# Retention scores in three float32r passes instead of one plain float32 product

## The chip, the cores and the metric

The kernel runs on one core of a Trainium2 chip. The metric is the device time of one execution in microseconds (us), from the core's first instruction to its last with what lies around them. Three executions give a median; one more was recorded by the hardware profiler.

## The reference

A decoder trunk of two layers over 512 tokens with 1024 channels. Each layer has a token mixer with three branches (retention, a gated recurrence called HGRN2, a Conformer convolution) and a feed-forward part with a convolution. The change is in the retention branch: 4 heads of 128 channels; queries and keys are rotated by position, and a token's output is the sum over earlier tokens of score x decay x value.

```python
def _rope(t, positions):
    ...
    return jnp.concatenate([t1 * cos - t2 * sin, t1 * sin + t2 * cos], axis=-1)

def _retention(q, k, v):
    """o_t = sum_{s<=t} gamma_h^(t-s) (q_t.k_s) v_s."""
    ...
        scores = jnp.einsum('bhtd,bhsd->bhts', qc, kc) * decay_mask
        out = jnp.einsum('bhts,bhsv->bhtv', scores, vc)
```

All inputs and outputs are float32. The kernel computes the scores over all earlier tokens at once instead of chunk by chunk.

## The kernel before, in words

Everything is held transposed: 128 channels on the partitions, 512 tokens along the free axis. A projection (`proj`) multiplies eight 128x128 weight tiles with eight 128x512 tiles of the input. Weights and inputs are split into two float32r parts: a high part rounded by ScalarE (`AF.Copy` into a float32r tile) and a low part, the difference, computed by VectorE. `mm3` (lines 248 to 251) then makes one product of three passes, high x high, high x low and low x high, which accumulate in PSUM. `split` (lines 226 to 232) does this for an intermediate result; `prefetch` (lines 215 to 217) does it for each 512 KB chunk of weights, with four buffers for the high and four for the low parts.

The order of the work is written by hand. The main loop runs projections. Heads are generators in a list `heads`, other work in a list `fill`. After every fourth weight tile `proj` calls `tick`, which takes one step of each of up to three heads and then steps of `fill` as a credit of microseconds allows. A head's TensorE instructions are put behind the last projection matmul by `issue_after(last[0].ins)`, where `last[0]` is set by `mm3`. Within these limits a planner in the compiler orders each engine's instructions by planned times; on the chip each engine takes them in that order.

In each layer, after the convolution inputs, the list `MIX` sets the order: values for HGRN2, two HGRN heads, values for retention, and then HGRN and retention heads mixed, with retention heads 2 and 3 last. For a retention head the main loop projects and rotates q, then projects and rotates k (`rope`, lines 536 to 543: two ScalarE copies that swap the halves, three VectorE operations), projects the gate, and appends `ret_head` (lines 545 to 562). That loads the decay mask (line 547); four steps follow, for key blocks j = 0 to 3, each with a score product of 128 keys with the w = 512, 384, 256 or 128 tokens from the block on (line 553) and a VectorE multiplication by the mask (line 555). Then four products with the values (line 561) and `head_out` give the branch's output.

The matmuls of the score products have plain float32 operands; in the profile each such product has two matmul records and two weight loads. The 47 buffers named `b` (tag "B") are shared by all such intermediate tiles, and the score products use one of two PSUM buffers `ps`.

Of the kernel before, what the change touches and what calls it, by code (L numbers as in the profile page):

```python
# [2 lines left out]

# [1 line left out]

# [14 lines left out]
S = 512  # L20
# [69 lines left out]
def trunk(ctx, tc, xT, cT, pos, ada, bada, wts, cols, lbl, rope_c, decay, hmask, outT):  # L90
    nc = tc.nc
    mm = nc.tensor.matmul
# [18 lines left out]
    def big(dt=F32, w=S):  # L111
        return bp.tile([P, w], dt, tag="B", name=nm("b"), bufs=NB)
# [7 lines left out]
    def pm():  # L120
        return pp.tile([P, S], F32, tag="pm", name=nm("pm"), bufs=4)

    def ps():
        return pp.tile([P, S], F32, tag="ps", name=nm("ps"), bufs=2)

    def po():
        return pp.tile([P, S], F32, tag="po", name=nm("po"), bufs=2)
# [36 lines left out]
    last = [None]  # L164
# [55 lines left out]
    def chunk(kind, ahead=LA):  # L220
        prefetch(ahead + 1 - len(ready))
        k, w = ready.pop(0)
        assert k == kind, (k, kind)
        return w

    def split(src, hi=None):
        if hi is None:
            hi = big(F32R)
            act(hi, src, AF.Copy)  # L229
        lo = big(F32R)  # L230
        tt(lo, src, hi.bitcast(F32), ALU.subtract)  # L231
        return hi, lo
# [15 lines left out]
    def mm3(dst, a, b, first, end):  # L248
        mm(dst, a[0], b[0], start=first, stop=False)  # L249
        mm(dst, a[0], b[1], start=False, stop=False)  # L250
        last[0] = mm(dst, a[1], b[0], start=False, stop=end)  # L251

    def sl2(w, o, n=128):
        return [t[:, o:o + n] for t in w]

    def proj(w, xs, us=TK):
        q = pm()
        n = len(xs)
        for k in range(n):
            mm3(q, sl2(w, 128 * k), xs[k], k == 0, k == n - 1)  # L260
            if k % 4 == 3:
                tick(us)
        return q

    def proj_octo(hs):
        qs = [pm(), pm(), pm(), pm(), ps(), ps(), po(), po()]
        for kt in range(KT):
            w = chunk("octo", 0)
            for n in range(8):
                mm3(qs[n], sl2(w, 128 * n), hs[kt], kt == 0, kt == KT - 1)  # L270
        return qs

    def proj_quad(kind, hs, between):

        qs = [ps(), pm(), ps(), pm()]
        ws = []
        for hf, (a, b) in enumerate(HALVES):
            for c in range(4):
                if hf == 0:
                    ws.append(chunk(kind, 0))  # L280
                for k in range(2):
                    kt = 2 * c + k
                    for n in range(4):
                        mm3(qs[n][:, a:b], sl2(ws[c], 512 * k + 128 * n), sl2(hs[kt], a, b - a),
                            hf == 0 and kt == 0, hf == 1 and kt == KT - 1)
                if hf == 0 and c == 0:
                    between()
        return qs
# [137 lines left out]
    def head_out(l, o, gname, h, sg, out):  # L426
        sq = big()
        act(sq, o, AF.Square)
        u = big()
        stt(u, o, col(l, gname, h), sg, ALU.mult, ALU.mult)  # L430
        sq = exact2(sq)
        yield 0.6
        for v in colsum(*sq):
            yield 0.0
        r = rstd(v, 8.0)
        tt(u, u, r, ALU.mult)
        out[h] = split(u)
        yield 3.0
# [97 lines left out]
    def rope(q, CC, SS):  # L536
        sw, o = big(), big()
        act(sw[0:64, :], q[64:128, :], AF.Copy)
        act(sw[64:128, :], q[0:64, :], AF.Copy)
        tt(o, q, CC, ALU.mult)  # L540
        tt(sw, sw, SS, ALU.mult)
        tt(o, o, sw, ALU.add)
        return o

    def ret_head(l, h, q, k, sg, v, out):
        dm = big()
        nc.sync.dma_start(dm, decay[h])
        yield 0.0
        pt = []
        for j in range(4):  # L550
            w = S - 128 * j
            z = ps()
            mm(z[:, 0:w], k[:, 128 * j:128 * (j + 1)], q[:, 128 * j:S], start=True, stop=True)  # L553
            a = big(w=w)
            tt(a, z[:, 0:w], dm[:, 0:w], ALU.mult)
            pt.append(a)
            yield 0.1 + w / 960
        o = po()
        hs = slice(128 * h, 128 * (h + 1))
        for j in range(4):  # L560
            mm(o[:, 128 * j:S], v[j][:, hs], pt[j], start=j == 0, stop=j == 3)  # L561
        yield from head_out(l, o, "retg", h, sg, out)
# [174 lines left out]
    for l in range(L):  # L737
# [20 lines left out]
        for what, h in MIX:  # L758
            if what == "g" and h < 0:
                for g, tp, q in proj_tok(hs):  # L760
                    for t2 in range(2):
                        act(vg[2 * tp + t2][:, 256 * g:256 * (g + 1)], q[:, 256 * t2:256 * (t2 + 1)], AF.Copy)
            elif h < 0:
                for g, tp, q in proj_tok(hs):
                    qv = q.rearrange("p (t h d) -> p t h d", h=2, d=128)
                    sm = bp.tile([P, 4], F32, tag="sm", name=nm("sm"), bufs=2)
                    nc.vector.tensor_reduce(sm, q.rearrange("p (a d) -> p a d", d=128),
                                            mybir.AxisListType.X, ALU.add)
                    for t2 in range(2):
                        stt(vr[2 * tp + t2][:, 256 * g:256 * (g + 1)].rearrange("p (h d) -> p h d", d=128),  # L770
                            sm[:, 2 * t2:2 * t2 + 2].unsqueeze(2).broadcast_to([P, 2, 128]), -1.0 / 128,
                            qv[:, t2], ALU.mult, ALU.add)
            elif what == "g":
                qf = proj(chunk("in"), hs)
                qq = proj(chunk("in"), hs)
                qg = proj(chunk("in"), hs)
                drain(heads, 2)
                heads.append(hgrn_head(l, h, *hgrn_gates(l, h, qq, qf, qg), vg, u_b))
            else:
                q = rope(proj(chunk("in"), hs), *CS)  # L780
                k = rope(proj(chunk("in"), hs), *CS)
                qg = proj(chunk("in"), hs)
                sg = big()
                act(sg, qg, AF.Silu)
                drain(heads, 2)
                heads.append(ret_head(l, h, q, k, sg, vr, u_a))

        ys = [None] * 8
        for bi, b in enumerate(ORDER):
            us = (u_a, u_b, u_c)[b]  # L790
            for jp in range(4):
                sg = []
                for t in range(2):
                    q = proj(chunk("in"), hs, TG if bi == 2 else TK)
# [9 lines left out]
                w = chunk("br")  # L804
                for t in range(2):
                    j = 2 * jp + t
                    q = pm()
# [16 lines left out]
        w = [chunk("out", 2), chunk("out", 1), chunk("out", 0)]  # L824
# [50 lines left out]
        for j in range(8):  # L875
# [4 lines left out]
            for a, b in parts:  # L880
                q = pm()[:, a:b]
                for k in range(FT):
# [3 lines left out]
                    w = [h[1] for h in held if h[0] == ci][0]  # L886
# [127 lines left out]
```

## Time and profile before

| What | Value |
| --- | --- |
| Median of 3 runs | 1808.3 us (1806.86 to 1808.81) |
| Profiled execution | 1809.82 us, of which the span in the trace is 1808.0 us |
| Granted TensorE clock, mean over the span | 0.998 |
| TensorE matmul, busy | 1781.2 us (99%) |
| VectorE, busy | 1297.0 us (72%) |
| ScalarE, busy | 761.9 us (42%) |
| GpSimd, busy | 35.3 us (2%) |

PE is TensorE's matmuls, PEld its weight loads, DVE VectorE, ACT ScalarE, POOL GpSimd. A matmul's duration in the trace includes the time in which the next one has already started, so the spacing of starts, and not the duration, is what a matmul costs. The chain of work that ended last is followed back from the last instruction; each of its pieces has the time by which it moved the end. The retention heads run from about 180 to 310 us in layer 0 and from about 1070 to 1210 us in layer 1.

### The profile page before, as it was taken

To read this page: it belongs to the slowest core of one execution; us is meant where nothing else is said; L and a number is where in the kernel's file an instruction comes from. 1 tells how busy PE (TensorE), PEld (TensorE's weight loads), DVE (VectorE), ACT (ScalarE), POOL (GpSimd) and SP (SyncE) were. 2 spreads that over 40 slices of the span, in tenths; PEclk is the share of its full clock that TensorE was granted. 3 is DMA by queue.
4 is the path that set the end of the run, shared out by engine and by line. 5 is a ranking of instruction groups with operands and counts; after the bars stand their busy time and mean duration, and the time that the engine had idled before them with its cause. 6 is when DMAs were issued, how large, how long until landed. Compare 5 with 4: busy or idle time off the path is not lost.

```text
span 1808.0 us, 25730 instructions
## 1 busy us (share of the span) xinstructions
PE 1781.2 (99%) x10308; PEld 1491.2 (82%) x10308; DVE 1297.0 (72%) x2169; ACT 761.9 (42%) x1074; POOL 35.3 (2%) x48
## 2 busy tenths in 40 slices
PE   7999999999999999999999999999999999999997
PEld 5888777888888888888889887778888988888886
DVE  6996576988779766667389666994885896666354
ACT  2444455334347444422273344552523564444222
POOL 3100000000000000000000000000000000000001
PEclk9999999999999999999999999999999999999999
DMA  8522222237634433255223222223583253223321
GB/s 299 184 81 82 77 83 76 94 117 228 218 91 139 140 103 96 94 186 187 89 95 105 72 88 72 70 87 97 191 271 106 82 163 128 94 94 101 97 82 47
DMA packets 63191, 217.27 MB, mean 120 GB/s; under 512 B 7392, under 2 KB 9824, under 8 KB 63072
## 3 DMA queue, kind: packets, MB, share of 16 engines
q1 hardware_dynamic: 63072, 215.63, 37.1%
q8 instruction: 81, 1.33, 0.3%
q14 instruction: 38, 0.31, 0.1%
HBM read 213.51 MB, written 2.10 MB: 119 GB/s over the span
## 4 chain that ended last, share of the span: by engine, by line
PE 91%; DVE 5%; DMA 2%; ACT 1%; issue 1%; SPq 0%; DVEq 0%; ACTq 0%
PE pm L249 28%; PE pm L251 27%; PE pm L250 27%; DMA ar<-ada 2%; DVE wl L217 1%; PE ps L553 1%; DVE ar L195 1%; PE po L561 1%; PE ps L481 1%; DVE x L664 1%; PE ps L250 1%; PE ps L251 1%; PE ps L249 0%; PE ps L474 0%; DVE h L688 0%
## 5 line engine op out<-in xcount | busy, mean ns | idle before, releaser
L249 PE MATMUL pm<-h,wh 128*128 128x512 f32 (+1 forms) x1568 | 611.7, 390 | 12.6 <-ACT wh L216 12.6
L251 PE MATMUL pm<-h,wl 128*128 128x512 f32 (+1 forms) x1568 | 604.0, 385 | 0.1
L250 PE MATMUL pm<-h,wh 128*128 128x512 f32 (+1 forms) x1568 | 602.6, 384 | 0.0
L217 DVE TENSOR_TENSOR wl<-wr,wh 128x1024 fp32r<-128x1024 f32 (+1 forms) x301 | 367.1, 1222 | 241.9 <-ACT wh L216 240.2
L216 ACT ACTIVATE wh<-wr 128x1024 fp32r<-128x1024 f32 (+1 forms) x301 | 317.1, 1056 | 499.3 <-PE pm L250 403.2
L249 PEld LDWEIGHTS pm<-h,wh 128*128 128x128 f32 x1568 | 295.3, 188 | 72.4 <-ACT wh L216 12.5
L251 PEld LDWEIGHTS pm<-h,wl 128*128 128x128 f32 x1568 | 295.1, 188 | 60.1 <-DVE wl L217 1.4
L250 PEld LDWEIGHTS pm<-h,wh 128*128 128x128 f32 x1568 | 295.3, 188 | 58.5 <-issue 1.7
L249 PE MATMUL pm<-b,wh 128*128 128x512 f32 (+1 forms) x764 | 279.0, 365 | 0.1
L250 PE MATMUL pm<-b,wh 128*128 128x512 f32 (+1 forms) x764 | 278.0, 364 | 0.6 <-DVE b L231 0.6
L251 PE MATMUL pm<-b,wl 128*128 128x512 f32 (+1 forms) x764 | 277.9, 364 | 0.0
L250 PEld LDWEIGHTS pm<-b,wh 128*128 128x128 f32 x764 | 144.1, 189 | 23.8 <-DVE b L231 0.9
L249 PEld LDWEIGHTS pm<-b,wh 128*128 128x128 f32 x764 | 144.2, 189 | 23.5 <-ACT b L229 0.5
L251 PEld LDWEIGHTS pm<-b,wl 128*128 128x128 f32 x764 | 144.1, 189 | 22.8
L383 DVE SCALAR_TENSOR_TENSOR b<-b,cols,b 128x511 f32<-128x511 f32 (+14 forms) x240 | 162.4, 729 | 0.0
L195 DVE SCALAR_TENSOR_TENSOR ar<-ar,cond 128x1024 f32<-128x1024 f32 x96 | 116.4, 1220 | 57.3 <-DMA ar<-ada 57.0
L229 ACT ACTIVATE b<-b 128x512 fp32r<-128x512 f32 x88 | 55.5, 630 | 196.2 <-DVE b L861 109.3
L231 DVE TENSOR_TENSOR b<-b,b 128x512 fp32r<-128x512 f32 x88 | 60.5, 688 | 32.2 <-ACT b L229 32.2
L249 PE MATMUL pm<-wh,h 128*128 128x256 f32 x256 | 73.9, 289 | 0.0
L250 PE MATMUL pm<-wl,h 128*128 128x256 f32 x256 | 72.3, 283 | 0.6 <-DVE wl L217 0.6
L251 PE MATMUL pm<-wh,h 128*128 128x256 f32 x256 | 72.3, 283 | 0.0
L854 ACT ACTIVATE b<-pm,cols 128x512 f32<-128x512 f32 x84 | 63.7, 761 | 0.8 <-PE pm L251 0.8
(224 smaller groups left out, 1686.5 us busy)
## 6 DMA issues: line engine op xcount, KB each, us to landing
wr<-wts SPq DMA_DIRECT2D x299, 512.0 KB, 3.5
ar<-ada SPq DMA_DIRECT2D x96, 512.0 KB, 4.4
x<-xT SPq DMA_DIRECT2D x8, 256.0 KB, 5.7
b<-decay SPq DMA_DIRECT2D x8, 256.0 KB, 3.8
outT<-b SPq DMA_DIRECT2D x16, 128.0 KB, 1.8
cond<-cT SPq DMA_DIRECT2D x1, 512.0 KB, 4.8
wr<-wts SPq DMA_DIRECT2D x2, 256.0 KB, 7.6
b<-pos SPq DMA_DIRECT2D x2, 256.0 KB, 4.3
```

What stands on the lines that cost most here:

```text
L195: stt(raw, raw, 1.0, cond, ALU.mult, ALU.mult, accum_out=dst)
L216: act(hi[:, s], raw[:, s], AF.Copy)
L217: tt(lo[:, s], raw[:, s], hi.bitcast(F32)[:, s], ALU.subtract)
L229: act(hi, src, AF.Copy)
L231: tt(lo, src, hi.bitcast(F32), ALU.subtract)
L249: mm(dst, a[0], b[0], start=first, stop=False)
L250: mm(dst, a[0], b[1], start=False, stop=False)
L251: last[0] = mm(dst, a[1], b[0], start=False, stop=end)
L383: stt(a[:, d:S], us[i][:, 0:S - d], col(l, "cw", 4 * (CK - 1 - d) + i0 + i), a[:, d:S], ALU.mult, ALU.add)
L481: mm(z[32 * r:32 * r + 32, 16 * i:16 * i + 16], ke[:, sl], rhs, start=True, stop=True)
L553: mm(z[:, 0:w], k[:, 128 * j:128 * (j + 1)], q[:, 128 * j:S], start=True, stop=True)
L854: act(a, q, AF.Identity, bias=col(l, "fb", i), scale=col(l, "fw", 88 + i))
```

## The change

The rotated q and k are no longer returned as float32 tiles but split into a high and a low float32r part. The score product goes through `mm3`: key tile high x query high, high x low, low x high. `keep_last` restores `last[0]` afterwards, so that the heads' instructions are still put behind the projections' matmuls and not behind the scores'. The product of the two low parts, which is not computed, is left out as in the other products in three passes. The product of scores and values (line 561) stays plain float32.

```diff
+    @contextmanager
+    def keep_last():
+        x = last[0]
+        yield
+        last[0] = x
...
         tt(o, q, CC, ALU.mult)
         tt(sw, sw, SS, ALU.mult)
         tt(o, o, sw, ALU.add)
-        return o
+        return split(o)
...
             z = ps()
-            mm(z[:, 0:w], k[:, 128 * j:128 * (j + 1)], q[:, 128 * j:S], start=True, stop=True)
+            with keep_last():
+                mm3(z[:, 0:w], sl2(k, 128 * j), sl2(q, 128 * j, w), True, True)
             a = big(w=w)
             tt(a, z[:, 0:w], dm[:, 0:w], ALU.mult)
```

## Rows read from the trace of the kernel before

**Rows 1.** The page: busy time and share of engines; the chain by engine.

```profile
PE 1781.2 (99%) x10308; PEld 1491.2 (82%) x10308; DVE 1297.0 (72%) x2169; ACT 761.9 (42%) x1074; POOL 35.3 (2%) x48
...
PE 91%; DVE 5%; DMA 2%; ACT 1%; issue 1%; SPq 0%; DVEq 0%; ACTq 0%
```

**Rows 2.** Waits of TensorE, whole run: total us, times, longest.

```profile
PE pm L249 <- ACT wh L216: 12.6, 1, 12.6
PE ps L250 <- DVE h L688: 1.6, 5, 0.3
PE pm L250 <- DVE wl L217: 0.6, 1, 0.6
PE pm L250 <- DVE b L231: 0.6, 1, 0.6
PE ps L249 <- ACT h L686: 0.6, 2, 0.3
```

**Rows 3.** Busy time by stretch, the two in which the heads run.

```profile
180.00:310.00 130.00, 129.93 (x951) 100.38 (x937) 83.92 (x155) 65.55 (x99) 0.73 (x2) 1.00 0.26 78
1070.00:1210.00 140.00, 140.00 (x1006) 108.44 (x1006) 117.39 (x211) 70.30 (x106) 0.68 (x2) 1.00 0.25 77
```

**Rows 4.** The chain in order of time, score products and one projection: start, us, piece.

```profile
180.57 0.38 PE ps L481 x32
180.95 0.43 PE pm L249
...
271.92 0.86 PE ps L553 x2
275.55 0.65 PE ps L553 x2
278.96 0.43 PE ps L553 x2
...
305.52 0.30 PE ps L553 x2
...
1142.58 1.05 PE ps L553 x2
```

**Rows 5.** Timeline of TensorE, a 128-column score product and its successor.

```profile
284.72 0.38 PE L553 MATMUL ps<-b,b 128*128 128x128 f32 x2
284.94 0.59 PE L561 MATMUL po<-b,b 128*128 128x512 f32 x1
```

**Rows 6.** Busy time by stretch: only 512-column passes, then only 256-column ones.

```profile
570.00:820.00 250.00, 250.00 (x1105) 207.01 (x1104) 167.83 (x235) 103.52 (x133) 0.00 (x0) 1.00 0.41 130
953.00:975.80 22.80, 22.80 (x192) 22.80 (x191) 22.80 (x33) 6.03 (x10) 0.00 (x0) 1.00 0.33 104
```

**Rows 7.** Timeline of TensorE and its weight loads in a projection.

```profile
196.95 0.39 PE L249 MATMUL pm<-h,wh 128*128 128x512 f32 x1
196.96 0.19 PEld L250 LDWEIGHTS pm<-h,wh 128*128 128x128 f32 x1
197.18 0.40 PE L250 MATMUL pm<-h,wh 128*128 128x512 f32 x1
```

**Rows 8.** The lines of `split`: durations in ns, min/median/max.

```profile
L229 ACT ACTIVATE b<-b x88: 611/632/636, 154.2 to 1704.6; 128x512 fp32r<-128x512 f32 x88
...
L231 DVE TENSOR_TENSOR b<-b,b x88: 680/691/693, 155.1 to 1705.3; 128x512 fp32r<-128x512 f32 x88
```

**Rows 9.** The page: the weights' high parts, and what ScalarE waited for.

```profile
L216 ACT ACTIVATE wh<-wr 128x1024 fp32r<-128x1024 f32 (+1 forms) x301 | 317.1, 1056 | 499.3 <-PE pm L250 403.2
```

**Rows 10.** Timeline, rotations' last sums and a first score product, layer 1.

```profile
1137.11 0.69 DVE L542 TENSOR_TENSOR b<-b,b 128x512 f32<-128x512 f32 x1
...
1183.97 0.68 DVE L542 TENSOR_TENSOR b<-b,b 128x512 f32<-128x512 f32 x1
...
1184.66 1.06 ACT L216 ACTIVATE wh<-wr 128x1024 fp32r<-128x1024 f32 x1 [3.95 <-PE pm L250]
...
1185.38 1.02 PE L553 MATMUL ps<-b,b 128*128 128x512 f32 x2
...
1185.75 1.23 DVE L217 TENSOR_TENSOR wl<-wr,wh 128x1024 fp32r<-128x1024 f32 x1 [0.46 <-ACT wh L216]
```

More of the change, by code (lines that the diff above doesn't have):

```diff
@@ L1 @@
 import math
-from contextlib import ExitStack
+from contextlib import ExitStack, contextmanager
 import numpy as np
```

## The prediction

> **What bounds the kernel now.** I began with the page's engine totals: TensorE is busy 1781.2 of 1808.0 us, VectorE 72%, ScalarE 42%, and 91% of the chain that ended last is TensorE [rows 1]. A busy TensorE is not yet a full one, so I asked next what it waits for. Over the whole run the waits above a tenth of a microsecond that the trace names come to 16 us, 12.6 of them one wait for the first weights [rows 2]; in the two stretches where the heads run, 180 to 310 us and 1070 to 1210 us, none of them falls. So there TensorE issues matmul behind matmul, and the time of these stretches is the sum of its matmuls' slots. VectorE is idle for 46 of the 130 us and 23 of the 140 us, ScalarE for 64 and 70 [rows 3]. The reader should see two things: a slot that the change takes from TensorE comes off the end nearly whole, and what it adds on the other two engines is free as long as TensorE does not begin to wait for it.
>
> **What it removes.** 32 plain float32 score products: 8 heads (4 in each of 2 layers), each with 512, 384, 256 and 128 columns. A matmul's own length in the trace overlaps its neighbours', so I take the price from the chain, which gives each piece only the time by which it moves the end: 0.86, 0.65 and 0.43 us for the three wide ones and 0.30 for a narrow one behind projections [rows 4]. Four of the eight 512-column ones show 1.05 or 1.06 us; those follow the HGRN head's small products, behind which a projection's pass too takes 0.43 us [rows 4] in place of its usual 0.23, so this 0.2 stays and I count 0.86 for all. The narrow one in front of the output product takes 0.22 (284.72 to 284.94 [rows 5]); between 0.22 and 0.30 I take 0.25. A head costs 0.86 + 0.65 + 0.43 + 0.25 = 2.19 us, eight heads 17.5 us.
>
> **What it puts there.** 96 float32r passes, three for each product. At 512 columns one takes 250.0 / 1105 = 0.226 us, at 256 columns 22.8 / 192 = 0.119 us [rows 6]. No float32r pass of 384 or 128 columns is in the trace. For 384 the straight line between the two rows gives 0.173, and both ends are close enough to leave it there. For 128 the ends are far apart: the line carried on gives 0.066 (low), a pass that gains nothing from being narrower than 256 costs 0.119, and a pass that is no faster than plain float32 at its width costs 0.25 (high; [rows 4, 5]). The nearest row in kind is the 256-column float32r one, so I take 0.119. A head then costs 3 x (0.226 + 0.173 + 0.119 + 0.119) = 1.91 us and saves 2.19 - 1.91 = 0.28 us; eight heads save 2.2 us. With the low end for the narrow pass a head saves 0.44 (3.5 us in all), with the high end it loses 0.11 (0.9 us lost). The whole edit on TensorE therefore lies between -3.5 and +0.9 us.
>
> Three passes also load weights three times where plain float32 loads twice. In the stream of projections a load of 0.19 us stands beside the matmul before it, and the matmuls still start 0.23 us apart [rows 7]; at 256 columns they start 0.119 apart, closer than a load lasts [rows 6]. So the passes' prices already hold their loads. The Trainium skill, in TensorE: Matmul & The Clock Gate, Part 3, The mechanism, says that a weight load overlaps a matmul in flight only when the two use different row groups, and under LDWEIGHTS it gives columns / 1.2 ns, 107 ns for 128. By it all 96 full-width passes would pay a load of their own, and the three passes of a 512-column product would take an estimated 3 x (0.213 + 0.107) = 0.96 us, more than the 0.86 removed. The trace's 0.23 us at full width does not bear that out.
>
> **What the split adds.** Each rotation now ends in a ScalarE copy (0.632 us) and a VectorE subtraction (0.691 us), like the other 88 splits [rows 8]. Two rotations a head make 16 of each: 10.1 us on ScalarE and 11.1 on VectorE, half of it in each stretch, 5.5 us against VectorE's idle 46 and 23. I cost that at nothing. What hides it is TensorE's matmul stream; without that cover it would be 21.2 us. What could be late behind it:
>
> The copy waits on ScalarE for the rotation's last sum, and behind it in ScalarE's order stand the next weights' copy and the next evictions. ScalarE now waits 403.2 us in all for TensorE to free a weight buffer before it may copy the next weights [rows 9], so weights are made as soon as one of the four buffers is free, some three chunks ahead of their use; a chunk is 24 matmuls, 24 x 0.226 = 5.4 us. A weight copy that comes 0.6 us later, or a subtraction 0.7 us later, is far inside that. The decay mask's load on SP's queue, and the output products, stay where they are.
>
> The score product itself waits for the split. For seven heads the last rotation's sum ends 4.7 us or more before the head's first product; the shortest of these is 1137.80 to 1142.5 [rows 4, 10]. A split of 0.63 + 0.69 = 1.3 us fits, even behind one weight copy and one weight subtraction (2.3 us more). For the last head of layer 1 it does not: the sum ends at 1184.65 and the product starts at 1185.38 [rows 10]. ScalarE has just taken a weight copy at 1184.66, so the key's copy would run from about 1185.7 to 1186.3; VectorE is in a weight subtraction until 1186.98, so the low part would come at about 1187.7. In the present order the first pass would wait 0.9 us and the third, two passes of 0.23 later, another 0.9: 1.8 us. The lower bound is nothing, if the order puts this product behind further projection matmuls, and that order is made anew from planned times. I take half, 0.9 us, once.
>
> Buffers: the split outlives the rotation, so each head holds two more of the 47 shared buffers. Following the program's order from first to last use I count at most 38 in use in this stage; with three heads at once that becomes some 44. No wait, so nothing; if the planner's order runs further ahead, a writer would wait for a free buffer, which belongs to the slow case below.
>
> **Sum.** -2.2 + 0.9 = -1.3 us. The profiled execution took 1809.82 us (span 1808.0 and 1.8 around it), so it would take 1808.5. The median of the runs shown is 1808.3, 1.5 below this execution, so the same change on the runs gives 1807.0.
>
> **Rivals.**
>
> *Narrow passes cost as plain float32.* For it: the kernel's float32r rows stop at 256 columns. Against it: nothing in this trace. The three passes of the 128-column product then take 0.75 for 0.25, all heads together lose 0.9, with 0 to 1.8 of the wait above: 1809.2 to 1811.0.
>
> *TensorE starts to wait for the other two engines* (the other side). Place: layer 1, where VectorE is busy 117.4 of 140 us [rows 3]. In-order VectorE takes the eight rotations' subtractions between the HGRN heads' updates and the weights' low parts; if it is behind there, TensorE stalls on a head's product. Price: at most a split's whole 1.32 us for each of 8 rotations, 10.6 us, less the 2.2 saved: +8.4, 1816.7. It decides by the bound below once 5.8 of the 10.6 us reach TensorE. For it: one such wait for a split's low part, 0.6 us, is in the trace, outside these stretches [rows 2]. Against it: that is the only one, and VectorE and ScalarE wait for TensorE far more than it does for them.
>
> *Loads not hidden.* If each of the 96 passes first paid the 0.19 us load of [rows 7] beside its columns, that would be 96 x 0.19 = 18.2 us, less the 2.2 saved: 1824. The 0.119 us starts speak against it. The overlap rule of the Trainium skill named above is this rival.
>
> *More is saved.* The narrow pass at the low end and no wait give -3.5; with a shift in the order that also closes some of the gaps behind the small products (0.2 us for each of four heads), -4.3, 1804.0. The bound asks for -3.6.
>
> That the change does nothing is not a rival: all 32 products go through the changed line.
>
> **Chances.** A difference of 0.2%, 3.6 us, is about what a measurement of this kernel can tell from none. My forecast (-2.2 to -0.4 us by the late product, widened by 1.0 on each side for the spread of the runs: -3.2 to +0.6) has 0.50, dear narrow passes 0.23, TensorE waiting 0.14 (0.12 of it beyond +3.6), unhidden loads 0.02, more saved 0.11. Faster is the last, 0.11; slower 0.12 + 0.02 + 0.01 from dear narrow passes with more than one late product = 0.15; the rest, 0.74, is same. The range goes from 1804.2, just short of the best case, to 1811.0, the top of the dear narrow passes; it leaves out most of the waiting and the unhidden loads (0.14) above and a third of the best case (0.04) below.
>
> **What would show it.** Right: in the chain a score product has three pieces of about 0.23, 0.17 and 0.12 us; TensorE's waits in the two stretches stay under 2 us, the largest at the last head of layer 1; ScalarE and VectorE gain 10 and 11 us of busy time; everything after 1210 us moves by the same amount. Wrong: narrow passes at 0.2 us or more; new waits of TensorE for the split or for weight parts in layer 1; or a shift that first shows outside the two stretches, which would mean that a new order of the work and not the price of the passes made the time.

## The result, and the profile after

The change made the kernel slower: 1817.62 us (median of 6 runs, 1816.5 to 1818.62) against 1808.14 us before (6 runs); the ratio is 1.0053, with a 95% interval of 1.0043 to 1.0063. That is 9.5 us more, where 1.3 us less was forecast. The profiled execution took 1818.23 us with a span of 1816.4 us; before's span was 1808.0.

The page of the kernel after, engine totals and chain, beside [rows 1]:

```profile
PE 1784.5 (98%) x10340; PEld 1495.5 (82%) x10340; DVE 1306.5 (72%) x2185; ACT 770.6 (42%) x1090; POOL 35.4 (2%) x48
...
PE 92%; DVE 5%; ACT 2%; DMA 1%; issue 0%; SPq 0%; DVEq 0%; ACTq 0%
```

VectorE has 9.5 us more work and ScalarE 8.7, about the 11 and 10 that the split was priced at. TensorE has 32 matmul records more: 96 passes in place of 64 records. None of these totals tells of a loss. To find where it lies, take an instruction that stands once at the end of each layer's token mixer and once at the end of each feed-forward part, the first matmul of the norm's pivot (a value that the norm subtracts from its input). First the kernel before, then after (count, durations in ns, first and last start in us):

```profile
L591 PE MATMUL ps<-b,avg_r x1: 404/404/404, 507.2 to 507.2; 128*128 128x512 f32 x1
L591 PE MATMUL ps<-b,avg_r x1: 404/404/404, 826.7 to 826.7; 128*128 128x512 f32 x1
L591 PE MATMUL ps<-b,avg_r x1: 404/404/404, 1398.3 to 1398.3; 128*128 128x512 f32 x1
```
```profile
L598 PE MATMUL ps<-b,avg_r x1: 404/404/404, 506.5 to 506.5; 128*128 128x512 f32 x1
L598 PE MATMUL ps<-b,avg_r x1: 404/404/404, 826.3 to 826.3; 128*128 128x512 f32 x1
L598 PE MATMUL ps<-b,avg_r x1: 404/404/404, 1406.7 to 1406.7; 128*128 128x512 f32 x1
```

(The second line is the norm at the end of layer 0's feed-forward part.) Layer 0 is 0.7 us ahead; 0.5 of that is a shorter first wait for weights (12.1 for 12.6 us). From 826 us to the pivot in layer 1 the kernel before takes 571.6 us and the kernel after 580.4: the loss of 8.8 us lies in layer 1's mixer. The six largest waits of TensorE over the whole run, beside [rows 2], point to it:

```profile
PE pm L249 <- ACT wh L216: 12.1, 1, 12.1
PE ps L249 <- DVE b L562: 3.7, 1, 3.7
PE ps L250 <- DVE h L695: 1.6, 5, 0.3
PE ps L249 <- ACT h L693: 0.8, 2, 0.6
PE po L243 <- ACT b L236: 0.8, 1, 0.8
PE pm L249 <- ACT b L791: 0.7, 1, 0.7
```

L562 is the mask multiplication (L555 before), and the 3.7 us stand in front of the last, 128-column score product of retention head 2 in layer 1. The timeline around it, TensorE and then VectorE:

```profile
1166.51 0.34 PE L251 MATMUL ps<-b,b 128*128 128x384 f32 x1
...
1191.44 0.33 PE L249 MATMUL ps<-b,b 128*128 128x128 f32 x1 [3.72 <-DVE b L562]
...
1191.83 2.15 PE L568 MATMUL po<-b,b 128*128 128x384 f32 x4
1193.65 0.80 PE L249 MATMUL pm<-b,wh 128*128 128x512 f32 x1
...
1202.59 0.63 PE L249 MATMUL pm<-b,wh 128*128 128x512 f32 x1
1203.02 0.63 PE L250 MATMUL pm<-b,wh 128*128 128x512 f32 x1
```
```profile
1189.10 1.22 DVE L217 TENSOR_TENSOR wl<-wr,wh 128x1024 fp32r<-128x1024 f32 x1
1190.23 0.69 DVE L231 TENSOR_TENSOR b<-b,b 128x512 fp32r<-128x512 f32 x1
1190.84 0.88 DVE L562 TENSOR_TENSOR b<-ps,b 128x384 f32<-128x384 f32 x2
```

The last pass of the 384-column product starts at 1166.51; VectorE multiplies it by the mask at 1190.84, 24.3 us later. I call this time the lag. Until then its PSUM buffer, one of two, is taken, and the fourth product needs it. The same place in the kernel before:

```profile
1167.70 0.48 PE L553 MATMUL ps<-b,b 128*128 128x384 f32 x1
...
1180.48 0.88 DVE L555 TENSOR_TENSOR b<-ps,b 128x384 f32<-128x384 f32 x2
...
1181.34 0.39 PE L249 MATMUL pm<-h,wh 128*128 128x512 f32 x1
1181.56 0.38 PE L553 MATMUL ps<-b,b 128*128 128x128 f32 x2
```

There the mask comes 12.8 us after its product, and the fourth product starts right behind a projection, 1.1 us after the mask began: no wait, but hardly any margin. The prediction did not use these rows.

After the wait TensorE is slow for a while. Busy time by stretch, after; the columns are TensorE's matmuls and loads, VectorE, ScalarE, GpSimd, then the granted clock, the DMA engines' busy share and their GB/s:

```profile
1180.00:1187.70 7.70, 7.70 (x35) 6.04 (x33) 7.70 (x12) 2.33 (x4) 0.00 (x0) 1.00 0.42 131
1187.70:1191.50 3.80, 0.08 (x2) 0.06 (x1) 3.80 (x7) 2.70 (x4) 0.00 (x0) 1.00 0.23 27
1191.50:1195.00 3.50, 3.50 (x10) 2.40 (x11) 3.50 (x7) 0.00 (x0) 0.00 (x0) 0.59 0.55 212
1195.00:1200.00 5.00, 4.17 (x19) 3.18 (x18) 4.71 (x9) 2.12 (x4) 0.00 (x0) 0.95 0.00 0
1200.00:1205.00 5.00, 4.08 (x11) 2.83 (x11) 5.00 (x9) 4.93 (x6) 0.00 (x0) 0.74 0.00 0
1205.00:1210.00 5.00, 5.00 (x21) 3.81 (x21) 5.00 (x8) 1.60 (x2) 0.00 (x0) 0.92 0.00 2
```

The granted clock averages 0.59 behind the idle 3.7 us, and 0.74 again from 1200 on; projection passes then start 0.43 us apart (1202.59 to 1203.02) and not 0.23: the lower of the two levels, 1.2 GHz for 2.4. The Trainium skill, in TensorE: Matmul & The Clock Gate, Part 1, says that the array's clock falls to half after idle time; the trace agrees, with 0.59 after the 3.72 us.

What this place costs: from the end of the last projection pass before the wait (1187.33 + 0.23) to the first pass at full rate (1205.79) TensorE spends 18.2 us. It does 26 passes of 512 columns (0.229 us each), the score passes of 128, 256 and 384 columns (0.35, 0.36 and 0.50 us) and output products (1.08 and 0.22 us), 8.5 us at the usual prices. So 9.8 us are lost here; less the 1.1 us that the passes were to save in a layer, that is about the 8.8 us of layer 1. The waits named are 3.7 + 0.8 + 0.2 + 0.7 = 5.5 us of it; most of the rest is the lower clock: what the granted clock lacks of 1 in the four stretches from 1191.5 on comes to an estimated 3.4 us of work at full speed.

### The profile page after: what moved, and what is told of

Read it like the earlier page. It is cut to its first block, busy times and chain, and to the rows that moved or that the text cites. A ratio compares the mean times of both kernels' runs of the same rounds, so it can differ in the third digit from the quotient of the medians.

```text
span 1816.4 us, 25820 instructions
## 1 busy us (share of the span) xinstructions
PE 1784.5 (98%) x10340; PEld 1495.5 (82%) x10340; DVE 1306.5 (72%) x2185; ACT 770.6 (42%) x1090; POOL 35.4 (2%) x48
## 4 chain that ended last, share of the span: by engine, by line
PE 92%; DVE 5%; ACT 2%; DMA 1%; issue 0%; SPq 0%; DVEq 0%; ACTq 0%
PE pm L249 29%; PE pm L251 28%; PE pm L250 28%; DVE wl L217 1%; PE po L568 1%; PE ps L487 1%; DVE x L671 1%; DVE ar L195 1%; PE ps L250 1%; PE ps L249 1%; PE ps L251 1%; ACT wh L216 1%; PE ps L480 0%; DMA wr<-wts 0%; DVE h L695 0%
## 5 line engine op out<-in xcount | busy, mean ns | idle before, releaser
L249 PE MATMUL pm<-h,wh 128*128 128x512 f32 (+1 forms) x1568 | 606.3, 387 | 12.1 <-ACT wh L216 12.1
L249 PEld LDWEIGHTS pm<-h,wh 128*128 128x128 f32 x1568 | 295.3, 188 | 69.3 <-ACT wh L216 12.1
L229 ACT ACTIVATE b<-b 128x512 fp32r<-128x512 f32 x104 | 65.5, 629 | 219.7 <-DVE b L868 109.1
L231 DVE TENSOR_TENSOR b<-b,b 128x512 fp32r<-128x512 f32 x104 | 71.6, 688 | 36.2 <-ACT b L229 36.2
L867 ACT ACTIVATE b<-b 128x512 f32<-128x512 f32 x44 | 27.8, 632 | 86.0 <-DVE b L863 83.5
```

Source lines behind the costliest of these rows:

```text
L867: act(t[0], t[0], AF.Silu)
```

## The experiments

Three theories stood at first. A: the split's VectorE work makes the mask late. B: the three passes, or the order planned around them, make the loss. C: the score product waits for the split's low part. All medians are of 4 to 11 runs; the kernel before was run on the same chip beside them.

**The two halves of the change.** `split_only`:

```diff
         tt(o, o, sw, ALU.add)
+        split(o)
         return o
```

> The rotated queries and keys are split as in the change (ScalarE copy, VectorE subtraction), but nothing reads the parts: the score products stay plain float32. Theory A (the 16 subtractions come in a stretch of layer 1 in which VectorE has no idle time, so a mask multiplication frees its PSUM buffer late and TensorE waits): slower than before by the whole 9.5 us of the change plus the 2.2 us that the passes no longer save, 1817 to 1821 us. Theory B (the three passes, or the order planned around them, make the loss): as before, 1807 to 1809. Theory C (the score product waits for the low parts): as before, because nothing waits for them.

Measured: 1819.02 us, ratio 1.0058 (1.0046 to 1.0071). The same wait is there:

```profile
1193.43 0.80 PE L554 MATMUL ps<-b,b 128*128 128x128 f32 x2 [5.20 <-DVE b L556]
```

`passes_only`:

```diff
-        sw, o = big(), big()
+        sw, o, r = big(), big(), big(F32R)
...
-        tt(o, o, sw, ALU.add)
-        return split(o)
+        tt(r, o, sw, ALU.add)
+        return r, r
```

> The rotation's last sum is written as float32r and used as both parts, so the score products have their three passes and there is no split (the scores are three times the high x high product). Theory A: the saving of the passes alone, 1805 to 1807 us. Theory B: the loss stays, 1815 to 1819. Theory C: 1805 to 1807.

Measured: 1805.44 us, ratio 0.9983 (0.9974 to 0.9992), and no wait of TensorE in the heads' stretches. So the whole loss comes with the split, also where nothing reads it, and the passes gain. B and C are out as causes of the change's loss.

**The split's parts.** `copy_only` adds only the ScalarE copy to the kernel before, `sub_only` only a VectorE subtraction of the same size:

```diff
         tt(o, o, sw, ALU.add)
+        act(big(F32R), o, AF.Copy)            # copy_only
+        tt(big(F32R), o, sw, ALU.subtract)    # sub_only
         return o
```

> Before, and each rotation also makes the ScalarE copy to float32r, which nothing reads; no subtraction, scores plain float32. Theory A (the loss is the subtractions' VectorE time in the part of layer 1 where VectorE has no idle time): as before, 1806 to 1810 us. Theory A2 (the copy delays ScalarE's evictions and weight copies) and theory D (any instruction more in the rotation makes the planner choose a worse order): 1815 to 1820.

> Before, and each rotation also makes one VectorE subtraction of 128x512 into a float32r tile that nothing reads; no ScalarE copy, scores plain float32. Theory A: the loss of split_only, 1815 to 1820 us, with a wait of TensorE of 3 us or more for a mask multiplication in layer 1. Theory A2: as before, 1807 to 1810. Theory D: 1815 to 1820 too, so this run tells A from A2, and copy_only tells A from D.

Measured: 1809.43 us (ratio 1.0012, 1.0003 to 1.0021) and 1809.73 us (the same ratio and interval). Theory A's number for `sub_only` was wrong: one part alone costs 1.4 to 2.2 us (by the medians and by the ratio), and no long wait appears. The timelines show why the two together are more than their sum. The lag from head 2's 384-column product in layer 1 to its mask (from here on counted from the product's first matmul record, which makes the change's 24.3 us 24.7) is 12.8 us in the kernel before, 18.4 us with the copy, 18.5 with the subtraction, 26.3 with both. TensorE comes to the fourth product 13.9, 19.5, 19.3 and 21.7 us after the second one began (21.6 in the change): up to about 21.5 us the order puts more projections in between, and beyond that a later mask, which itself takes 0.6 us, is waited for. `sub_twice` (two subtractions, no copy) was to tell this from a theory D, that the planner orders badly when both parts are there:

> Before, and each rotation makes two VectorE subtractions that nothing reads, no ScalarE copy, plain float32 scores. One such subtraction lengthened the lag of the third retention head's second mask multiplication from 12.8 to 18.5 us without a wait. Theory A: a second one brings it to some 24 us and a wait of TensorE appears, 1814 to 1822 us. Theory D: no wait without the ScalarE copy, 1809 to 1812.

Measured: 1814.8 us, ratio 1.0035 (1.0023 to 1.0048). The lag is 21.6 us, and TensorE waits 1.0 us for the mask:

```profile
PE ps L555 <- DVE b L557: 1.0, 1, 1.0
```

The granted clock falls there as well, to a mean of 0.57 over 1198 to 1202 us. TensorE gets to the fourth product 21.2 us after the second began, as in the kernels above. So a loss of this kind doesn't need the copy. The copy's 5.6 us of lag, on the other hand, are no VectorE time of its own: counted from the pivot at the end of layer 0, seven convolution taps (96 for 89) and two weight subtractions more than before stand ahead of this mask in VectorE's order.

**Is it the PSUM buffer, or the mask?** `shared_bank` puts the third and fourth product into one buffer in one step:

```diff
-        for j in range(4):
-            w = S - 128 * j
-            z = ps()
+        for js in ((0,), (1,), (2, 3)):
+            z, c = ps(), 0
+            for j in js:
...
+                    mm3(z[:, c:c + w], sl2(k, 128 * j), sl2(q, 128 * j, w), True, True)
```

> The whole change, but the products of 256 and 128 columns go into one PSUM buffer in one step, before their two mask multiplications, so that the fourth product needs no buffer of its own. Theory A1 (the wait is for a free PSUM buffer and nothing else needs the late mask soon): the wait goes, 1804 to 1810 us. Theory A2 (the mask multiplication itself is too late): the wait moves to the output product, which reads the masked scores, and the time stays at 1814 to 1820.

Measured: 1816.0 us, ratio 1.0045 (1.0033 to 1.0058). The wait moved to the output product, which reads the masked scores, and kept its size:

```profile
1189.40 0.88 DVE L567 TENSOR_TENSOR b<-ps,b 128x384 f32<-128x384 f32 x2
```
```profile
1190.00 2.50 PE L574 MATMUL po<-b,b 128*128 128x384 f32 x4 [3.68 <-DVE b L567]
```

So a further buffer alone would hardly have helped: the mask itself is late.

**Taking the wait away.** Six attempts, five of them on VectorE's load. `sub_on_gpsimd` runs the 16 subtractions on GpSimd (`ptt(lo, o, hi.bitcast(F32), ALU.subtract)`):

> The whole change, but the rotations' 16 subtractions run on GpSimd, which is idle in this stage. Theory A: the loss goes and the saving stays, 1805 to 1808 us, if the GpSimd work doesn't slow VectorE's own. Theory B: 1815 to 1819. Theory C: the low parts come later than on VectorE, so at least the loss of the change, 1817 to 1825.

Measured: 1817.27 us, ratio 1.0045 (1.0032 to 1.0057). A's number failed, but not by the old wait, which is down to 0.7 us in three pieces. New ones took its place:

```profile
PE ps L487 <- DVE b L500: 2.7, 4, 0.8
PE ps L251 <- POOL b L551: 2.5, 3, 0.9
...
PE po L571 <- DVE b L436: 1.3, 1, 1.3
```

GpSimd takes 1.6 us for a subtraction, so here theory C does hold: the third pass waits for the low part, three times. The run says little about A.

`taps_credit_1p5` asks for more credit per step of the convolution taps, the largest filler of VectorE in this stretch:

```diff
-            yield 1.2
+            yield 1.5
```

> The whole change, and each step of the convolution's taps asks for a credit of 1.5 us in place of 1.2 (its two VectorE instructions take 1.46), so that fewer of them are put between the heads' work in layer 1. Theory A: VectorE is less behind, the wait shrinks or goes, 1805 to 1811 us. Theories B and C: 1815 to 1819, since TensorE's passes and the split are as in the change.

Measured: 1834.37 us, ratio 1.014 (1.0126 to 1.0154), above every range named. The mask's wait is gone, but the taps end too late: the third branch's input is not ready and TensorE waits 13.4 us for its split (L229), 10.4 of them in layer 0, whose pivot comes at 524.6 us and not at 506.5. `taps_later_l1` therefore changes layer 1 alone and gives the taps more room after the heads (`yield 1.2 if l == 0 else 1.45 if heads else 1.0`); `before_taps_later_l1` is its control.

> The whole change; in layer 1 a step of convolution taps asks for a credit of 1.45 us in place of 1.2 while heads are open, and of 1.0 after them; layer 0 as in the change. Theory A (VectorE's lag behind TensorE in layer 1 makes the wait, whatever the lag is made of): no wait for a mask multiplication, the saving of the passes stays, 1804 to 1808 us. Theory D (copy and subtraction together make the planner choose a bad order): the wait stays, 1814 to 1820.

> The kernel before with the same credits of the taps in layer 1 and nothing else: the control for taps_later_l1. Before has no wait to lose, so both theories say 1806 to 1810 us; if it is faster than before by more than 2 us, a gain of taps_later_l1 is not all due to the wait.

Measured: 1810.53 us (ratio 1.0013, 1.0005 to 1.0022) and 1809.86 us (1.0011, 1.0002 to 1.002). No wait for a mask is left, and VectorE has idle time in the stretch (13.6 us busy of the 20 from 1160 on), but theory A's 1804 to 1808 us is missed. The loss shrinks from 9.5 to 2.4 us, and 1.8 of these belong to the taps' new credit. But the change on top of the control is 0.7 us slower, not 2.2 faster. The lag is 13.3 us although VectorE idles for a third of that time.

`charge_head` lets a head's first step ask for 1.3 us of credit, and `gates_on_scalar` moves the HGRN gates' eight tensor-scalar operations of layer 1 to ScalarE (theory E is that the planner's order spreads the loss over the stage):

> The whole change, and a retention head's first step asks for a credit of 1.3 us in place of 0, for its two subtractions, so that eight pairs of convolution taps or so come later in a layer. Theory A: VectorE is less behind in layer 1, and the wait for the mask multiplication goes in part or whole: 1805 to 1813 us. Theory D: no rule; near the change, 1814 to 1820.

> The whole change, and the HGRN heads' eight tensor-scalar operations of layer 1 run on ScalarE, which takes about 4 us from VectorE in that layer, some 1 us of it after 1110 us. Theory A: the lag and the wait shrink a little, 1811 to 1817 us. Theory E: no rule; 1812 to 1820, so this run is weak alone.

Measured: 1821.85 us (1.0078, 1.0065 to 1.0091) and 1818.32 us (1.0057, 1.0043 to 1.007). Both miss theory A's range: the lag of the late mask stays at 24.1 and 25.9 us, with waits of 3.5 and 5.2 us. In `charge_head` the time beyond the change's is lost in layer 0, whose pivot comes at 510.8 us (506.5 in the change). In `gates_on_scalar` VectorE has 4.1 us of gates less, but 102 taps stand ahead of the late mask where the change has 98: the order used up what was freed. Small relief on VectorE does not reach the mask.

`product_later_l1` leaves all work as in the change and gives the head two more ticks before its fourth product, in layer 1; `before_product_later_l1` is the control.

```diff
             yield 0.1 + w / 960
+            if l and j == 2:
+                yield 0.0
+                yield 0.0
```

> The whole change; in layer 1 a retention head lets two ticks pass between its third and its fourth score product, so that TensorE has up to 5.5 us more of projections before it needs the late mask multiplication. VectorE's work is that of the change. Theory A (the loss is TensorE's wait for the lagging mask and the clock that falls after it): the wait goes, 1804 to 1809 us. Theory E (the loss is spread over the stage by the planner's order, and the wait is only where it shows): 1812 to 1820.

> The kernel before with the same two ticks: the control. Before has no wait there, so both theories say 1806 to 1810 us.

Measured: 1807.55 us (ratio 0.9996, 0.9987 to 1.0005) and 1807.98 us (0.9999, 0.999 to 1.0008). With the same instructions the 10 us are gone, and E with them. But the edit did not act as it was meant to. VectorE and TensorE in this run:

```profile
1174.34 0.89 DVE L562 TENSOR_TENSOR b<-ps,b 128x384 f32<-128x384 f32 x2
```
```profile
1166.37 0.34 PE L251 MATMUL ps<-b,b 128*128 128x384 f32 x1
...
1178.53 0.27 PE L251 MATMUL ps<-b,b 128*128 128x128 f32 x1
```

TensorE comes to the fourth product not later but 12 us after the second (21.6 us in the change, where it then waits), and the mask 8.0 us after its product's last pass (24.3 in the change): the planner made another order, in which the mask stands ahead of the previous head's four normalisation steps and not behind them. VectorE is as full as before, 20.0 of the 20 us from 1160 on. So the order of VectorE's queue, and not its load alone, sets how late the mask is.

**A kernel that beats both.** `one_pass` writes the rotation's last sum as float32r and makes one pass for each score product:

```diff
-        sw, o = big(), big()
+        sw, o, r = big(), big(), big(F32R)
...
-        tt(o, o, sw, ALU.add)
-        return o
+        tt(r, o, sw, ALU.add)
+        return r
```

> The rotation's last sum is written as float32r and the score product is one float32r pass (the low parts are left out of the scores). VectorE and ScalarE do what they did before, TensorE has 8 x (2.19 - 0.64) = 12.4 us less. Theory A: most of that is gained, 1796 to 1800 us, less what VectorE's lag gives back: TensorE reaches the mask multiplications earlier, so up to 4 us may be lost to waits. If the passes or their operand type made the loss (theory B): 1808 or more.

Measured: 1796.49 us, ratio 0.9936 (0.9924 to 0.9949): 11.5 of the 12.4 us that the passes were priced at. It gives up the low parts of queries and keys, which the change is there to keep.

## Why the prediction was wrong

**What bounds the kernel** held: `passes_only` and `one_pass` show that TensorE's slots come off the end nearly whole.

**The passes** held. The 384- and 128-column passes, for which 0.173 and 0.119 us were taken, stand like this in the kernel after (starts in us; the next start ends the slot):

```profile
253.16 0.33 PE L250 MATMUL ps<-b,b 128*128 128x384 f32 x1
253.32 0.34 PE L251 MATMUL ps<-b,b 128*128 128x384 f32 x1
...
261.49 0.27 PE L250 MATMUL ps<-b,b 128*128 128x128 f32 x1
261.60 0.27 PE L251 MATMUL ps<-b,b 128*128 128x128 f32 x1
261.71 0.45 PE L251 MATMUL pm<-h,wl 128*128 128x512 f32 x1
```

0.16 to 0.19 at 384 columns (0.19 at 1166.51) and 0.11 at 128: the narrow float32r pass is no dearer per pass than the 256-column one, and the dear narrow passes, a rival with 0.23, did not happen. The saving was forecast at 2.2 us; `passes_only` measured 3.2, with an interval of 1.4 to 4.7. The rival of unhidden loads is out with it.

**The step that failed** is the one that cost the split on VectorE at nothing. It set 5.5 us of subtractions against 23 idle us of a 140 us stretch [rows 3]. The same view of the kernel before in shorter stretches shows what that mean hid (the third busy time is VectorE's):

```profile
1070.00:1120.00 50.00, 50.00 (x479) 38.34 (x479) 30.25 (x63) 23.94 (x39) 0.68 (x2) 1.00 0.23 73
1120.00:1140.00 20.00, 20.00 (x221) 15.42 (x220) 19.05 (x42) 10.20 (x15) 0.00 (x0) 1.00 0.21 68
1140.00:1160.00 20.00, 20.00 (x98) 15.64 (x99) 19.00 (x33) 10.34 (x22) 0.00 (x0) 1.00 0.32 95
1160.00:1170.00 10.00, 10.00 (x43) 7.64 (x42) 10.00 (x16) 4.36 (x6) 0.00 (x0) 1.00 0.31 103
1170.00:1180.00 10.00, 10.00 (x44) 7.86 (x43) 10.00 (x16) 4.09 (x6) 0.00 (x0) 1.00 0.16 52
```

20 of the 23 idle us lie before 1120. From there to 1180 VectorE is idle for 2 of 60 us, in the stretch in which heads 1 and 2 and the queries of head 3 are rotated. What would then be late was missed too: the prediction asked who waits for the split (its own score product), not who stands behind it in VectorE's queue. Behind it stood the mask multiplications, and TensorE needs those twice over, for the PSUM buffer and for the masked scores.

**The late product** at the last head, priced at 0.9 us, did not occur: that product came at 1196.46, behind projections.

**The rival on the other side**, TensorE waiting for the other engines in layer 1, had the right place and nearly the right time, 1816.7 us, at a chance of 0.14. Its price was made otherwise, though: 10.6 us of the splits' own time, of which every us would have reached TensorE. That was called the most that it could be; between `passes_only` and the change lie some 12 us. What the runs show is a threshold. One part of the split brings the lag from 12.8 to 18.5 us and costs 1.4 to 2.2 us; both bring it to 25 or 26, past the 21.5 us or so of work that TensorE has in hand there, and then a wait of 4 to 5 us comes with a lower clock behind it, some 10 us in all.

**How much of the delay is the split's own time** can be counted from what VectorE did ahead of the mask. From the pivot at 826 us to the late mask, first before and then after, the convolution taps (length, VectorE's busy us and count, then clock and DMA):

```profile
826.70:1180.40 353.70, 60.59 (x89) 1.00 0.29 93
826.30:1190.80 364.50, 66.56 (x98) 1.00 0.30 94
```

and the subtractions of `split` (L231):

```profile
826.70:1180.40 353.70, 3.93 (x6) 1.00 0.29 93
826.30:1190.80 364.50, 8.80 (x13) 1.00 0.30 94
```

The mask comes 10.8 us later. The seven subtractions of the rotations are 4.9 us of that; nine more taps (6.0 us) and two more weight subtractions (2.3 us), which the change does not add but the new order puts ahead of the mask, are the rest (their ends overlap a little, and VectorE idles 1.5 us less). So the time that the prediction left out is under half of the delay, and the planner's order is the larger part.

**Open** is why the planner orders the taps so; no run held the order fixed and added the split. `product_later_l1` is 0.8 us faster than before, with an interval from 2.4 us faster to 0.9 slower that just holds the forecast 2.2, and gains less than the passes alone. The traces say where the rest is lost. From the pivot at 826 us to that of layer 1 `product_later_l1` takes 570.2 us, as little as `passes_only` with 570.6. In layer 0, from the first matmul of L487 (L481 before) to the pivot, `passes_only` takes 399.3 us, `product_later_l1` 400.5, the change 400.6 and before 401.4. So the split costs some 1.2 us in layer 0 as well, without a long wait; why is not shown.

## What to carry to other kernels

Before work is called hidden on a second engine, look at that engine's idle time in stretches as short as the work in question, and list what stands behind the new instruction in its queue and who waits for that. For an instruction that frees a buffer of the bounding engine, read the lag from producer to consumer and the work that the bounding engine has until it needs the buffer: here 12.8 us of lag stood against 13.9 us of work, which grew to 21 or 22 in the runs that waited and no further. Where an order is planned anew at each edit, try the whole change in another order before the edit itself is blamed: the same instructions took 1817.6 and 1807.6 us.

## What the runs showed of the hardware that I had not expected

The granted clock fell a second time, to a mean of 0.74 over 1200 to 1205 us, after waits of 0.8, 0.2 and 0.7 us, none near the 3.7 us before the first fall. In `sub_twice`, where no wait near it is longer than 1.0 us, it fell too (0.57 over 1198 to 1202 us). A subtraction of two 128x512 float32 tiles to float32r took 1.6 us on GpSimd against 0.69 on VectorE:

```profile
L551 POOL TENSOR_TENSOR b<-b,b 128x512 fp32r<-128x512 f32 x16 | 25.4, 1585 | 254.3 <-ACT b L550 254.3
```
